# Queries, keys and gates by seven block products in a stage of their own, the attention and scan branches exchanged

## The chip, the cores and the metric

One core of a Trainium2 chip runs the whole program. The time is the device time of one execution in microseconds (us); the profile's span is the time from the first to the last instruction of one profiled execution. TensorE (PE in the profile) multiplies matrices, with PEld for the loading of its stationary operand; VectorE is DVE, ScalarE is ACT, GpSimd is POOL, and SyncE (SP) issues most DMA transfers. ScalarE and GpSimd issue some transfers as well.

## The reference

One decoder layer over 512 tokens of width 1024, in fp32: two parallel branches on the normalised input, merged by gates, then a SwiGLU feed-forward. Cut to what matters here:

```python
xn = rmsnorm(x, norm1_w)                       # (512, 1024)
q, k, v, z, xbc, dt_raw, gate_logits = split(xn @ w_in)   # 1536 | 1536 | 1536 | 2048 | 3072 | 32 | 2048
# attention branch: 3 dilation groups x 8 heads of 64, window of 128 steps
for g, (window, dil) in enumerate(((128, 1), (512, 4), (2048, 16))):
    o_g, lse_g = dilated_window_attention(q[:, :, g], k[:, :, g], v[:, :, g], bias[g], dil, window // dil)
attn = sum_g softmax_g(lse_g) * o_g            # (512, 512)
# scan branch (Mamba-2 SSD): 32 heads of 64 in 4 groups, state 128, chunks of 128
xbc = silu(causal_conv4(xbc)); dt = softplus(dt_raw + dt_bias)
y = ssd_chunked_scan(xs, dt, -exp(a_log), B, C) + xs * d_skip
ssm = grouped_rmsnorm(y * silu(z)) * ssm_norm_w
gates = sigmoid(gate_logits)                   # two of width 1024
merged = gates[0] * (attn @ w_attn_branch) + gates[1] * (ssm @ w_ssm_branch)
h = x + merged @ w_out
h = h + (silu(g) * u) @ w_ffn_out              # g, u = split(rmsnorm(h, norm2_w) @ w_ffn_in)
return rmsnorm(h, final_norm_w)
```

## The kernel before

Everything is held transposed: features on the 128 partitions, the 512 tokens along a row. To keep fp32 accuracy in a faster matmul format, each operand is split into a high part (rounded copy, made by ScalarE) and a low part (the difference, made by VectorE); a product is then three matmuls, high x high, high x low and low x high. This is `project` (L238): one block of 128 output features, 8 input blocks of 128, 24 matmuls of 128x512 into one PSUM bank. `values` (L311) does the same for V with tokens on the partitions: a group of 512 features takes 4 chunks (`c`) of 4 token blocks (`tt`), 6 matmuls each.

Weights stream through `Weights` (L45): a list of chunks in the order of use (`_chunk_plan`, L1204), loaded two chunks ahead by SP, split one chunk ahead (`fill`, L71: high part on ScalarE L81, low part on VectorE L82), with three buffers for raw, high and low parts.

The order of the work, by stage:

1. Start (to about 52 us). x is loaded, split unnormalised (`xu`), and V of group 0 is made from it, scaled per token when evicted (`keep`, L482). Woven between its token blocks by the table `at`: column sums, the root, its spread over rows (`first_rows`), the step sizes (`steps` L418, `steps_by_token` L429), the normalised input `xn` (`normalised`, L466). Then the first B and C blocks. In this stage the instructions of TensorE, VectorE and ScalarE keep the order in which they are written.
2. Scan (about 52 to 399 us). Four groups; in each a B and a C block, then four times an X and a Z block. `pair` (L547) is the scan of two heads and advances step by step at hooks: `project` calls one at its middle and one at its end. After group 2 come eight half blocks of the scan's output projection, `ssm_half(j, 0)`; after group 3 V of group 1.
3. V of group 2, the second halves `ssm_half(j, 1)`, then attention (about 499 to 677 us): for each of four pairs of heads, six blocks (query and key for three groups), whose results are split straight out of PSUM, and `softmax_pair` (L717), a generator of six steps: scores of group 0; scores of groups 1 and 2 and an exchange of row maxima through DRAM; exponentials and an exchange of sums; transposes (two steps); products with V. It advances at the end of each block. Eight gate blocks follow, and eight times a gate block and an attention branch block (four input blocks), which give `merged`.
4. The output projection, and the feed-forward's input: `Pairs` (L92) does two blocks of 128x1024 weights at once as a 2x2 arrangement of submatrices with seven products instead of eight (a Strassen-Winograd scheme): the tokens' halves and the features' halves give eight right-hand factors (`B11` to `B12`, `T1` to `T4`), the weights' halves and their sums (`sums13`, `sums24`) the left ones. Each product is 12 matmuls of 128x256. Low parts of unsummed weights are made by an accumulating DMA that GpSimd issues (`added`, L116): ScalarE writes the negated high part, the transfer adds the weights from DRAM. Then the feed-forward's output and the last norm.

Outside the hand-ordered parts a planner orders each engine's instructions by priority of writing and readiness, on its own estimate of durations; buffers are given out from pools and wait for their last readers. The lines of the start that the change's weave replaces:

```python
at = {(1, 1): column_sums, (1, 2): first_root, (2, 0): first_rows,
      (2, 1): lambda: (normalised(range(0, 4)), steps()),
      (2, 3): lambda: (steps_by_token(), normalised(range(4, 6))),
      (3, 1): lambda: normalised(range(6, 8)),
      (3, 3): lambda: ([next(chain) for _ in range(6)], nc.sync.dma_start(v_t[0], v0))}
```

Of the kernel before, what the change touches and what calls it, by code (L numbers as in the profile page):

```python
# [9 lines left out]
F32 = mybir.dt.float32  # L10
# [18 lines left out]
OUT_ORDER = (0, 4, 1, 5, 2, 6, 3, 7)  # L29

# [14 lines left out]
class Weights:  # L45


    def __init__(self, nc, pool, chunks, dma_ahead=2, split_ahead=1):
        self.nc, self.pool, self.chunks = nc, pool, chunks
        self.da, self.sa = dma_ahead, split_ahead  # L50
        self.i = self.loaded = self.split = 0
        self.raw, self.parts = {}, {}
# [18 lines left out]
    def fill(self, ahead=None, between=None):  # L71
        self.load(ahead)
        while self.split < min(len(self.chunks), self.i + (self.sa if ahead is None else ahead) + 1):
# [5 lines left out]
            for ks in self.pieces(i, kt):  # L79
                cs = slice(ks.start * n, ks.stop * n)  # L80
                self.nc.scalar.activation(hi[:, cs], r[:, cs], AF.Copy)  # L81
                self.nc.vector.tensor_sub(lo[:, cs], r[:, cs], hi[:, cs])  # L82
                if between:
                    between.pop(0)()
# [84 lines left out]
def trunk(ctx: ExitStack, tc: tile.TileContext, xT, w_in, w_v, w_dt, w_attn, w_ssm, w_out, w_fi, w_fo,  # L169
# [41 lines left out]
    wst = Weights(nc, wp, _chunk_plan(w_in, w_v, w_attn, w_ssm, w_out))  # L211
# [26 lines left out]
    def project(ps, rhs, first=True, last=True, at=None, w=wst):  # L238
        h, l, kt = w.next()
        for k in range(kt):  # L240
# [4 lines left out]
            if at is not None:  # L245
                if k in at:
                    at[k]()
            elif k == 3 and kt == KD:
                hook(False)
        if at is None:  # L250
            hook(True)
# [38 lines left out]
    def rel_rows(pool):  # L290

        tiles = [[pool.tile([P, S], F32, tag=f"sbr{2 * g + i}", name=f"rel{i}_{g}") for i in range(2)] for g in range(3)]
        for g in range(3):
            nc.gpsimd.dma_start(tiles[g][0][:33, : LREL[g]], oneh_d[:, OREL[g] : OREL[g] + LREL[g]])
        yield
        for g in range(3):
            (oneh, rv), n = tiles[g], LREL[g]
# [31 lines left out]
    sbr_cm = tc.tile_pool(name="sbr", bufs=1, reuse_waits="tile")  # L329
    sbrp = sbr_cm.__enter__()  # L330
# [3 lines left out]
    hcw = ssc.tile([P, P], F32, name="hcw")[:, :96]  # L334
    hcb = ssc.tile([P, 96], F32, name="hcb")[:, :24]
    relb = ssc.tile([33, 32], F32, name="relb")[:, :24]
    dt, la, te, eE = [ssc.tile([P, P], F32, name=n) for n in ("dt", "la", "te", "eE")]
# [4 lines left out]
    v_t = [v.rearrange("(c p) d -> p c d", p=P) for v in v_d]  # L342

    xn_cm = tc.tile_pool(name="xn", bufs=1, reuse_waits="tile", side="right")
    xnp = xn_cm.__enter__()

    order = tc.manual_schedule(engines={mybir.EngineType.PE, mybir.EngineType.DVE, mybir.EngineType.Activation})
    order.__enter__()
    with tc.tile_pool(name="s0", bufs=1, reuse_waits="tile") as s0:
        xt = [s0.tile([P, S], F32, name=f"x{k}") for k in range(KD)]  # L350
        xu = [tuple(s0.tile([P, S], F32R, name=f"xu{n}{k}") for n in "hl") for k in range(KD)]
        v0 = s0.tile([P, NCH, S], F32, name="v0")
        laf = s0.tile([32, S], F32, name="laf")
        t128 = s0.tile([P, S], F32, name="t128")
        ssum = s0.tile([P, S], F32, name="ssum")
        col = s0.tile([P, 32], F32, name="col")
        v, ab, e, ri, ss, s2, h, dta = [s0.tile([P, P], F32, name=f"c{i}") for i in range(8)]
        ax = s0.tile([P, 32], F32, name="ax")
        wd = s0.tile([P, KD, 32], F32, name="wd")
        sid = s0.tile([P, 64], F32, name="sid")  # L360
        rb1 = s0.tile([P, S], F32, name="rb1")
# [20 lines left out]
        act.activation(v[:, :NCH], mhalf, AF.Exp)  # L382
# [26 lines left out]
        ch = lambda t: t.rearrange("p (c h) -> p c h", h=32)  # L409
# [19 lines left out]
        def steps_by_token():  # L429
# [3 lines left out]
            for c in range(NCH):  # L433
                ev.scalar_tensor_tensor(v[:, c * 32 : c * 32 + 32], pt[:, c * 64 : c * 64 + 32], r1[0][:, c : c + 1],
                                        par("dtb", 0, 32), op0=ALU.mult, op1=ALU.add)

        def softplus():
            ev.scalar_tensor_tensor(ab, v, -1.0, v, op0=ALU.mult, op1=ALU.max)
            act.activation(e, ab, AF.Exp, scale=-1.0)
            act.activation(ax, par("alog", 0, 32), AF.Exp)  # L440
            yield
            ev.tensor_scalar(v, v, 0.0, None, op0=ALU.max)
            yield
            ev.tensor_scalar(ri, e, 2.0, None, op0=ALU.add)
            yield
            ev.reciprocal(ri, ri)
            yield
            ev.tensor_mul(ss, e, ri)
            yield
            ev.tensor_mul(s2, ss, ss)  # L450
            yield
            ev.tensor_scalar(h, s2, 1.0 / 15, None, op0=ALU.mult)
            for c in (13, 11, 9, 7, 5, 3):
                yield
                ev.scalar_tensor_tensor(h, h, 1.0 / c, s2, op0=ALU.add, op1=ALU.mult)
            yield
            ev.scalar_tensor_tensor(h, h, 1.0, ss, op0=ALU.add, op1=ALU.mult)
            yield
            ev.scalar_tensor_tensor(dt, h, 2.0, v, op0=ALU.mult, op1=ALU.add)
            yield  # L460
            ev.scalar_tensor_tensor(ch(dta), ch(dt), -1.0, ax.unsqueeze(1).to_broadcast([P, NCH, 32]), op0=ALU.mult, op1=ALU.mult)

        xn = []
        xm, todo = {}, []

        def normalised(ks):  # L466
            for k in ks:
                xm[k] = s0.tile([P, S], F32, tag="xm", name=f"xm{k}", bufs=3)
# [3 lines left out]
                xn.append((hi, lo))  # L472
                act.activation(hi, xm[k], AF.Copy)
                todo.append(k)
                while len(todo) > (k < KD - 1):
                    i = todo.pop(0)
                    (gp if i % 2 else ev).tensor_sub(xn[i][1], xm[i], xn[i][0])
# [4 lines left out]
        def keep(tt):  # L482
            act.activation(v0[:, tt, :], pv[tt], AF.Copy, scale=r1[0][:, tt : tt + 1])

        def decays():
            pl = bank()
            mm(pl[:, :P], tri, dta)
            mm(pl[:, P : 2 * P], ones, dta, start=False)
            act.activation(la, pl[:, :P], AF.Copy)
            act.activation(eE, pl[:, P : 2 * P], AF.Exp)  # L490
            ev.tensor_sub(te, pl[:, P : 2 * P], la)
            act.activation(te, te, AF.Exp)

        def decay_rows():
            pf = bank()
            for c in range(NCH):
                pe.transpose(pf[:32, c * P : c * P + P], la[:, c * 32 : c * 32 + 32], ident)
            act.activation(laf, pf[:32, :], AF.Copy)
            gp.dma_start(la_d, laf)
            dump("dt", dt)  # L500
            dump("la", laf)

        chain = softplus()
        at = {
            (1, 1): column_sums,
            (1, 2): first_root,
            (2, 0): first_rows,
            (2, 1): lambda: (normalised(range(0, 4)), steps()),
            (2, 3): lambda: (steps_by_token(), normalised(range(4, 6))),
            (3, 1): lambda: normalised(range(6, 8)),  # L510
            (3, 3): lambda: ([next(chain) for _ in range(6)], nc.sync.dma_start(v_t[0], v0)),
# [3 lines left out]
        pb0 = project(bank("mm"), xn, at={0: lambda: [None for _ in chain]})  # L515
        pc0 = project(bank("mm"), xn, at={4: decays, 7: decay_rows})
    order.__exit__(None, None, None)

    holder = {}
# [18 lines left out]
    with tc.tile_pool(name="sp", bufs=1, reuse_waits="tile") as sp:  # L538
# [109 lines left out]
        for g in range(NG):  # L648
# [14 lines left out]
            if g == 0:  # L663
                slow.append(rel_rows(sbrp))
# [646 lines left out]
```

## Time and profile before

| | us |
|---|---|
| median of three runs | 1147.26 (1146.73 to 1152.67) |
| profiled execution | 1150.79 |
| its span | 1149.0 |
| PE busy | 1132.8 |
| DVE busy | 715.3 |
| ACT busy | 569.9 |
| POOL busy | 181.6 |

The mean granted TensorE clock is 0.996. PE's busy time is 99% of the span; matmuls are pipelined, so busy means that one was under way, not that the array was full. The DMA engines moved 142.35 MB, a mean of 124 GB/s. Rows of busy time by stage have the stretch, its length, then for each engine busy us and the number of instructions, the granted clock, the share of the 16 DMA engines' time and GB/s.

### The profile page before, as it was taken

What the parts mean: (1) busy time and instruction counts of PE and PEld (TensorE: products, weight loads), DVE (VectorE), ACT (ScalarE), POOL (GpSimd) and SP (SyncE); (2) the same over time, 40 slices, a digit from 0 to 9 for tenths busy, and PEclk for the clock granted to TensorE, in tenths of its full rate; (3) what the DMA queues carried; (4) which work ended last, traced back from release to release, by engine and by line L of the source; (5) the groups of instructions that cost most, each with busy time, mean ns of one, the idle gap of its engine ahead of it and who ended that gap; (6) DMA issues with size and microseconds to landing.
All of it is one profiled execution on the core that took longest, in us unless ns stands there. A gap on an engine that the chain in (4) does not pass through costs nothing.

```text
span 1149.0 us, 17104 instructions
## 1 busy us (share of the span) xinstructions
PE 1132.8 (99%) x6636; PEld 969.5 (84%) x6636; DVE 715.3 (62%) x1253; ACT 569.9 (50%) x997; POOL 181.6 (16%) x169
## 2 busy tenths in 40 slices
PE   9999999999999999999999999999999999999996
PEld 6777888878888788888888888888999999988886
DVE  5777897873579333455564534478888777773222
ACT  5555565554345331336536533356767667663321
POOL 3214313222013300011211100000111111100001
PEclk9999999999999999999999999999999999999999
DMA  6343333233332373332333224345688888844322
GB/s 220 130 149 98 121 94 111 92 111 110 92 92 74 110 256 96 106 93 75 93 85 83 63 90 123 112 151 171 148 184 186 191 193 186 172 129 129 101 65 74
DMA packets 51521, 142.35 MB, mean 124 GB/s; under 512 B 6439, under 2 KB 13119, under 8 KB 51184
## 3 DMA queue, kind: packets, MB, share of 16 engines
q1 hardware_dynamic: 42096, 120.90, 33.9%
q0 software_dynamic: 6896, 16.04, 8.4%
q10 hardware_dynamic: 2448, 4.32, 1.3%
q8 instruction: 52, 0.85, 0.3%
q14 instruction: 29, 0.24, 0.1%
HBM read 133.76 MB, written 7.48 MB: 123 GB/s over the span
## 4 chain that ended last, share of the span: by engine, by line
PE 91%; DVE 4%; DMA 2%; ACT 1%; issue 1%; POOL 0%; SPq 0%; ACTq 0%; DVEq 0%; POOLq 0%
PE mm L179 74%; PE aux L179 15%; PE aux L182 2%; DVE wlo L82 1%; DMA x<-xT 0%; DMA lab<-la_d 0%; DVE frl L950 0%; DMA h_d<-h 0%; ACT whi L81 0%; DVE fS_lo L138 0%; DMA fa<-w_fi 0%; DVE xm L469 0%; DVE h L958 0%; POOL n2r L273 0%; DVE fA_lo L131 0%
## 5 line engine op out<-in xcount | busy, mean ns | idle before, releaser
L82 DVE TENSOR_TENSOR wlo<-wraw,whi 128x1024 fp32r<-128x1024 f32 (+2 forms) x156 | 185.7, 1195 | 185.3 <-ACT whi L81 185.1
L81 ACT ACTIVATE whi<-wraw 128x1024 fp32r<-128x1024 f32 (+2 forms) x156 | 152.2, 981 | 267.1 <-PE mm L179 238.1
L179 PE MATMUL mm<-xnh,whi 128*128 128x512 f32 x640 | 251.8, 393 | 1.4 <-DVE acc L530 1.3
L179 PE MATMUL mm<-xnh,wlo 128*128 128x512 f32 x640 | 252.6, 395 | 0.0
L179 PE MATMUL mm<-xnl,whi 128*128 128x512 f32 x640 | 251.1, 392 | 0.0
L179 PEld LDWEIGHTS mm<-xnh,whi 128*128 128x128 f32 x640 | 120.3, 188 | 27.3 <-ACT ce L562 1.7
L179 PEld LDWEIGHTS mm<-xnh,wlo 128*128 128x128 f32 x640 | 120.2, 188 | 26.9 <-issue 2.7
L179 PEld LDWEIGHTS mm<-xnl,whi 128*128 128x128 f32 x640 | 120.2, 188 | 24.9 <-issue 1.2
L179 PE MATMUL mm<-hhl,whi 128*128 128x512 f32 (+1 forms) x171 | 62.6, 366 | 0.6 <-DVE hhl L259 0.6
L179 PE MATMUL mm<-hhh,whi 128*128 128x512 f32 (+1 forms) x171 | 62.8, 368 | 0.2 <-ACT hhh L258 0.2
L179 PE MATMUL mm<-hhh,wlo 128*128 128x512 f32 (+1 forms) x171 | 62.3, 365 | 0.0
L121 POOL DMA_DIRECT2D fD_lo<-w_fi x22 | 19.1, 866 | 246.3 <-DVE h L958 135.8
L563 POOL TENSOR_TENSOR ce<-ce,Cf 128x768 f32<-128x768 f32 x16 | 34.7, 2173 | 140.9 <-ACT ce L562 78.2
L530 DVE SCALAR_TENSOR_TENSOR acc<-mm,hcw,acc 128x511 f32<-128x511 f32 (+2 forms) x72 | 53.2, 743 | 1.0
L138 DVE TENSOR_TENSOR fS_lo<-s,fS_hi 128x1024 fp32r<-128x1024 f32 x44 | 52.0, 1217 | 0.0
L179 PE MATMUL mm<-ssml,whi 128*128 128x512 f32 x128 | 50.2, 392 | 0.0
L179 PE MATMUL mm<-ssmh,wlo 128*128 128x512 f32 x128 | 50.1, 392 | 0.0
L179 PE MATMUL mm<-ssmh,whi 128*128 128x512 f32 x128 | 49.9, 390 | 0.0
L179 PE MATMUL mm<-frh,fS_hi 128*128 128x256 f32 x176 | 49.4, 281 | 0.5 <-ACT c L1031 0.5
L179 PE MATMUL aux<-frh,fS_hi 128*128 128x256 f32 x176 | 49.4, 280 | 0.0
L179 PE MATMUL aux<-frl,fS_hi 128*128 128x256 f32 x176 | 49.1, 279 | 0.0
L179 PE MATMUL aux<-frh,fS_lo 128*128 128x256 f32 x176 | 49.1, 279 | 0.0
(320 smaller groups left out, 2571.1 us busy)
## 6 DMA issues: line engine op xcount, KB each, us to landing
wraw<-w_in SPq DMA_DIRECT2D x80, 512.0 KB, 3.6
fb<-w_fi SPq DMA_DIRECT2D x22, 512.0 KB, 3.7
fa<-w_fi SPq DMA_DIRECT2D x22, 512.0 KB, 5.0
fA_lo<-w_fi POOLq DMA_DIRECT2D x19, 512.0 KB, 5.8
lab<-la_d SPq DMA_DIRECT2D x16, 512.0 KB, 3.7
wraw<-w_ssm SPq DMA_DIRECT2D x16, 512.0 KB, 3.8
wraw<-w_fo SPq DMA_DIRECT2D x15, 512.0 KB, 3.6
wraw<-w_v SPq DMA_DIRECT2D x11, 512.0 KB, 3.7
```

The source lines that it names most:

```text
L81: self.nc.scalar.activation(hi[:, cs], r[:, cs], AF.Copy)
L82: self.nc.vector.tensor_sub(lo[:, cs], r[:, cs], hi[:, cs])
L121: self.nc.gpsimd.dma_start(lo.rearrange("p (k n) -> p k n", n=P), src, accum_op=ALU.add)
L138: self.nc.vector.tensor_sub(lo, t, hi)
L179: pe.matmul(out, lhsT, rhs, start=start, stop=stop, skip_group_check=True)
L182: pe.transpose(out, src, ident)
L530: ev.scalar_tensor_tensor(acc[:, d:], ps[:, : S - d], hcw[:, t * 4 + 3 - d : t * 4 + 4 - d], acc[:, d:], op0=ALU.mult, op1=ALU.add)
L563: gp.tensor_mul(ce, ce, Cf[:, P:].unsqueeze(1).to_broadcast([P, 2, S - P]))
```

## The change

- Queries, keys and gates leave `project`. They are 20 pairs (12 of a query and a key block, 8 of the two gates' blocks) in a new loop with the feed-forward's `Pairs`, `product` and `head`, seven products of 12 matmuls a pair, between the start and attention. Only TensorE's order is written out there. Results go to DRAM: queries and keys already split and permuted (`qk_d`, 4 x 512 a partition), gates after their tanh (`gate_d`, 2 x 512).
- The start makes V of groups 0 and 1 from the unnormalised input. `normalised` now writes a column's low part right after its high part, all on VectorE; `factors` makes the token factors T1 to T4. Three of V's chunks get their low parts by accumulating DMA. The first B and C blocks leave the start. The softplus of the steps moves into the pairs' loop.
- Attention comes before the scan. `load_heads` brings a head pair's queries and keys back with 16 transfers; V of group 2, six of the sixteen Z blocks (`EARLY_Z`, results kept in DRAM) and the first B and C blocks are woven with it; `attention` advances the four generators at every hook, two of them interleaved.
- The scan has no Z blocks for tiles 8 to 13; the first half of its output projection comes at tiles 10 and 11; the attention branch's blocks are at its end, with the gates loaded from DRAM; the second half of the output projection gives `merged`.

The diff, cut to its core (moved code is left out):

```diff
+EARLY_Z = range(8, 14)
+HALF_AT = {10: (0, 1, 2), 11: (3, 4, 5, 6, 7)}
...
-            for ks in self.pieces(i, kt):
+            if i in self.added:
+                self.nc.scalar.activation(hi, r, AF.Copy)
+                self.nc.scalar.activation(lo, hi.bitcast(F32), AF.Copy, scale=-1.0)
+                self.nc.gpsimd.dma_start(lo.rearrange("p (k n) -> p k n", n=n), self.chunks[i], accum_op=ALU.add)
+            for ks in self.pieces(i, kt) if i not in self.added else ():
...
-    wst = Weights(nc, wp, _chunk_plan(w_in, w_v, w_attn, w_ssm, w_out))
+    wst = Weights(nc, wp, [w_v[g, c] for g in (0, 1) for c in range(4)], added=(5, 6, 7))
...
         def normalised(ks):
             for k in ks:
-                xm[k] = s0.tile([P, S], F32, tag="xm", name=f"xm{k}", bufs=3)
+                xm[k] = s0.tile([P, S], F32, tag="xm", name=f"xm{k}", bufs=4)
                 ev.scalar_tensor_tensor(xm[k], xt[k], par("n1", k), rb1, op0=ALU.mult, op1=ALU.mult)
...
                 act.activation(hi, xm[k], AF.Copy)
-                todo.append(k)
-                while len(todo) > (k < KD - 1):
-                    i = todo.pop(0)
-                    (gp if i % 2 else ev).tensor_sub(xn[i][1], xm[i], xn[i][0])
+                ev.tensor_sub(lo, xm[k], hi)
+
+        def factors(p):
+            f = s0.tile([P, 4, HS], F32, tag="tf", name=f"tf{p}", bufs=2)
+            (b11, b12), (b21, b22) = [[xm[k][:, :HS], xm[k][:, HS:]] for k in (p, p + 4)]
+            hi, lo = tw[p]
+            ev.tensor_sub(f[:, 0], b11, b12)
+            ev.scalar_tensor_tensor(f[:, 1], b22, -1.0, f[:, 0], op0=ALU.mult, op1=ALU.subtract)
+            ev.tensor_sub(f[:, 2], b22, b12)
+            ev.scalar_tensor_tensor(f[:, 3], f[:, 1], -1.0, b21, op0=ALU.mult, op1=ALU.subtract)
+            act.activation(hi, f, AF.Copy)
+            ev.tensor_sub(lo, f, hi)
...
+            (0, 3): column_sums,
+            (1, 0): first_root,
+            (1, 2): first_rows,
+            (1, 3): steps,
+            (2, 0): lambda: normalised((0, 4)),
+            (2, 2): lambda: (steps_by_token(), normalised((1, 5))),
+            (3, 0): lambda: (factors(0), wst.fill(1)),
+            (3, 2): lambda: (normalised((2,)), factors(1)),
+            (3, 3): lambda: (nc.sync.dma_start(v_t[0], v01), wst.fill(1)),
...
+            (0, 0): lambda: normalised((6,)),
+            (0, 1): lambda: (factors(2), wst.fill(1)),
+            (0, 3): lambda: normalised((3, 7)),
+            (1, 1): lambda: (factors(3), ev.tensor_copy(r1[1], r1[0])),
+            (1, 2): lambda: wst.fill(1),
+            (1, 3): first_pairs,
+            (2, 3): lambda: holder["fi"].first(0, add=False),
+            (3, 0): lambda: holder["fi"].sums13(0),
+            (3, 1): lambda: holder["fi"].load(1),
+            (3, 2): lambda: holder["fi"].first(1, add=False),
+            (3, 3): lambda: (holder["fi"].sums24(0), holder["fi"].sums13(1), nc.sync.dma_start(v_t[1], v01)),
...
+    def finished(n, i, src):
+        if n < 12:
+            if i == 0:
+                outs[n] = p1.tile([P, 4, S], F32R, tag="st", name=f"st{n}", bufs=2)
+            st = outs[n]
+            parted((st[:, 2 * i], st[:, 2 * i + 1]), src, 1.0 if i else -0.125, n % 3)
+            if i:
+                nc.sync.dma_start(qk_d[n], outs.pop(n).bitcast(F32))
+        else:
...
+            act.activation(st[:, i], src, AF.Tanh, scale=-0.5 if i else 0.5)
+            if i:
+                nc.sync.dma_start(gate_d[n - 12], outs.pop(n)[:, :2])
...
+    for n in range(NP):
...
+        r, q, c1, c5 = heads.pop(n)
...
+        fi.last(n)
...
+        product(s_, fi, factor, n, "a12", B21, True, True)
+        ev.tensor_add(ga[:, half[0]], s_, c1)
...
+        fi.sums13(n + 1)
+        product(r, fi, factor, n, "s2", T2, False, False)
+        u2 = copied(p1, r, "u2", n)
+        if before:
+            finish1(*before)
+        product(q, fi, factor, n, "s4", B22, False, True)
+        ev.tensor_add(ga[:, half[1]], q, u2)
+        fi.load(n + 2)
+        fi.sums24(n + 1)
+        product(r, fi, factor, n, "s3", T3, False, False)
...
+        finished(n, 0, ga)
...
+        quick.append([attention()])
         for c in range(4):
             values(pv, 2, c, xn, stage2)
+        for t in EARLY_Z:
+            ps = project(bank("mm"), xn)
...
+            nc.sync.dma_start(zs_d[t], z)
+        pb0 = project(bank("mm"), xn)
+        pc0 = project(bank("mm"), xn)
+        drain()
...
+                if t in EARLY_Z:
+                    nc.sync.dma_start(zs[t], zs_d[t])
...
+                for j in HALF_AT.get(t, ()):
+                    first_half(j)
...
         for j in range(KD):
+            t = sp.tile([P, 2, S], F32, tag="lab", name=f"gt_{j}", bufs=2)
+            nc.sync.dma_start(t, gate_d[j])
+            ev.scalar_tensor_tensor(sbr[j], t[:, 0], 1.0, sbr[j], op0=ALU.add, op1=ALU.mult)
+            pa = project(bank("mm"), attn)
+            ev.scalar_tensor_tensor(t[:, 1], t[:, 1], 1.0, pa, op0=ALU.add, op1=ALU.mult)
+            ev.tensor_add(sbr[j], sbr[j], t[:, 1])
```

800 lines of the change are left out of this document (436 added, 364 removed).

## The prediction

> **What bounds the kernel now.** I read the page's head and its chain first, then busy time by stage, then the chain in order of time.
>
> ```profile
> span 1149.0 us, 17104 instructions
> PE 1132.8 (99%) x6636; PEld 969.5 (84%) x6636; DVE 715.3 (62%) x1253; ACT 569.9 (50%) x997; POOL 181.6 (16%) x169
> PE 91%; DVE 4%; DMA 2%; ACT 1%; issue 1%; POOL 0%; SPq 0%; ACTq 0%; DVEq 0%; POOLq 0%
> ```
>
> TensorE is busy 99% of the span and carries 91% of the chain. So matmul time removed is time saved, unless TensorE then waits for what it did not wait for before. The stages (columns: length, then busy us of PE, PEld, DVE, ACT, POOL, granted clock, DMA share, GB/s) tell how near the others are:
>
> ```profile
> 0.00:39.00 39.00, 36.19 (x168) 26.47 (x169) 23.33 (x38) 20.36 (x31) 13.75 (x15) 0.96 0.47 162
> 52.00:288.70 236.70, 235.36 (x1337) 188.88 (x1336) 182.35 (x336) 128.92 (x253) 65.32 (x40) 1.00 0.35 113
> 499.00:677.50 178.50, 178.50 (x1062) 151.34 (x1061) 94.95 (x240) 91.37 (x212) 23.67 (x34) 1.00 0.30 78
> 825.00:995.00 170.00, 170.00 (x1446) 170.00 (x1445) 136.11 (x228) 120.28 (x176) 29.57 (x35) 1.00 0.83 188
> ```
>
> Rows two and three are the scan and the attention with its projections: VectorE is 77% busy in the one, 53% in the other. The last is the feed-forward, which already uses the seven products: weight loads fill it wholly, VectorE is at 80%, ScalarE at 71%, the DMA engines at 83%. The new stage has that shape.
>
> **Part 1: seven products for eight, a gain of 20.0 us.**
>
> ```profile
> 673.18 76.22 PE mm L179 x336
> 841.87 1.41 PE aux L179 x12
> 851.76 1.41 PE aux L179 x12
> 583.47 5.49 PE mm L179 x24
> 628.33 5.49 PE mm L179 x24
> ```
>
> Chain rows: start, length, what. 336 matmuls in 76.22 us are 0.2268 us each, so a block of 24 takes 5.44 and the two blocks of a pair 10.89. A feed-forward pair, 7 x 12 = 84 matmuls of half the columns, takes 851.76 - 841.87 = 9.89. Half the columns cost 0.118, not 0.113, since each also loads weights. So a pair saves 1.00, not an eighth of 10.89, and 12 pairs of queries and keys with 8 of gates save 20.0. Values, Z, B, C, X, the branch and output blocks keep their count and are costed at nothing where they only move.
>
> **Part 2: the start, a loss of 17 us.** Before, four chunks of values end at 39.09 and two ordinary blocks follow. After, group 1's four chunks run there (21.8 us, to 60.9), and in their cover VectorE and ScalarE, in the written order, must make the normalised columns, the four factors and the weight parts.
>
> ```profile
> 27.53 1.92 PE L179 MATMUL aux<-x,wd 128*32 128x512 f32 x16
> 39.09 0.39 PE L179 MATMUL mm<-xnh,whi 128*128 128x512 f32 x1
> 23.07 1.23 DVE L82 TENSOR_TENSOR wlo<-wraw,whi 128x1024 fp32r<-128x1024 f32 x1
> 26.88 1.42 DVE L469 SCALAR_TENSOR_TENSOR xm<-x,prm,rb 128x512 f32<-128x512 f32 x2 [2.58 <-ACT rb L480]
> 28.33 0.69 DVE L477 TENSOR_TENSOR xnl<-xm,xnh 128x512 fp32r<-128x512 f32 x1
> 33.81 0.73 DVE L434 SCALAR_TENSOR_TENSOR c<-aux,n1r,prm 128x32 f32<-128x32 f32 x4 [1.81 <-PE aux L179]
> 899.82 0.41 DVE L1103 TENSOR_TENSOR us<-us,g 128x256 f32<-128x256 f32 x1
> 27.66 1.29 ACT L473 ACTIVATE xnh<-xm 128x512 fp32r<-128x512 f32 x2 [0.82 <-DVE xm L469]
> 31.97 0.58 ACT L422 ACTIVATE t<-aux 128x512 f32<-128x512 f32 x1
> 36.43 1.04 ACT L81 ACTIVATE whi<-wraw 128x1024 fp32r<-128x1024 f32 x1
> fA_lo<-w_fi POOLq DMA_DIRECT2D x18, 512.0 KB, 5.9
> ```
>
> The row at 33.81 shows the order binding: VectorE sits idle 1.81 us for TensorE with four columns still to normalise. Where before the low part of a column came after the next column's product, after it follows its own high part at once: 0.71 + 0.64 (ScalarE, VectorE waiting) + 0.69 and two hand-overs, 2.15 a column. A factor is 4 x 0.41, then the high part of 1024 (1.04), then the low (1.23): 4.1 with hand-overs.
> The walk: the steps' matmuls move up past two token blocks (2 x 1.36), so they end at 27.53 - 2.7 + 1.9 = 26.7, and ScalarE's copy of them (0.58) now stands ahead of a weight split (1.04 + 1.23). The first column starts near 29.6. Eight columns (17.2), four factors (16.4), the steps (0.73) and one split with its wait (1.7) end at 65.6, past 60.9. Worse, the parts of the last three value chunks are issued by ScalarE behind factors 0, 2 and 3 (two copies of about 1.05, then an accumulating transfer of 5.9 to landing). Chunk 6 stands behind the high part of factor 2, at 29.6 + 6 x 2.15 + 0.73 + 1.7 + 2 x 4.1 + 2.8 = 55.9, and lands at 63.9; TensorE wants it at 39.1 + 10.9 = 50. Chunk 7 lands near 72, so the values end near 77 instead of 60.9. Queued behind on ScalarE are the values' evictions and, behind these, the sums of the first two pairs: another 4 to 5 us before the second pair's first sum. The upper end is 21. The lower: VectorE never waits, 8 x 1.40 + 4 x 2.9 + 2.4 = 25 us from 29.6, done near 55, leaves about 3 for the sums. I take 17, near the upper end because the row at 33.81 is of that kind, less some for transfers that land sooner where DMA is at 0.47 than at 0.83.
>
> **Part 3: DMA in the pairs of queries and keys, a loss of 5 us.** Added on SP's queue: per such pair a store of 1.05 MB, per gate pair 0.52.
>
> ```profile
> q0 software_dynamic: 5115, 14.02, 47.9%
> q1 hardware_dynamic: 6018, 18.23, 33.8%
> 10.00:15.00 5.00, 5.00 (x16) 3.91 (x16) 4.74 (x6) 5.00 (x9) 2.97 (x2) 0.66 1.07 378
> 415.00:420.00 5.00, 5.00 (x24) 4.14 (x23) 0.75 (x1) 2.70 (x4) 0.00 (x0) 1.00 1.01 371
> ```
>
> The queue rows are of 825 to 1000 us. Of 9.89 us a pair, accumulation takes 47.9% (4.74) and loads 33.8% (3.34): 8.1. A store at 371 GB/s adds 2.8; at the loads' own rate (18.23 MB in 0.338 x 175 us, 308 GB/s) 3.4. That is 10.9 to 11.5 of DMA time, and a share of 1.07 is the highest shown: 10.2 at best, so 0.3 to 1.6 over TensorE's 9.89, or 4 to 19 over 12 pairs. Stores of 8 KB a row are nearest the 371 row: 10.9 / 1.05 = 10.4, thus 5 to 6, and I take 5. Gate pairs need about 9.5 and fit. A store queues ahead of the next pair's loads, which the sums on VectorE wait for. The rest of a pair's work is the feed-forward's: its tanh and two products give way to two splits of 512.
> The Trainium skill, "DMA: Bandwidth & Descriptors", the table at its head, gives HBM about 358 GB/s for one core. By that a pair's 2.9 MB need 8.1 us, the store hides and this part is 0; the trace differs on both counts, since loads ran at 371 and accumulation at 14.02 MB in 83.8 us, 167 GB/s.
>
> **Part 4: attention woven with other blocks, a loss of 3 us.**
>
> ```profile
> L780 ACT ACTIVATE L<-L,nm 128x256 f32<-128x256 f32 x32 | 15.8, 496 | 13.2 <-DVE nm L771 13.2
> L777 ACT ACTIVATE L<-L,nm 128x256 f32<-128x256 f32 x24 | 11.9, 497 | 0.0
> L777 ACT ACTIVATION_READ_ACCUMULATOR L<-L,nm 128x1 f32 x32 | 6.1, 190 | 0.0
> L780 ACT ACTIVATION_READ_ACCUMULATOR L<-L,nm 128x1 f32 x32 | 6.0, 187 | 0.0
> dscr<-d POOLq DMA_DIRECT2D x4, 4.0 KB, 1.7
> d1n<-dscr POOLq DMA_DIRECT2D x4, 4.0 KB, 3.7
> L913 DVE SCALAR_TENSOR_TENSOR sbr<-g,sbr 128x512 f32<-128x512 f32 x6 | 4.1, 685 | 0.0
> ```
>
> A head pair took 628.33 - 583.47 = 44.86 with six blocks of 5.44, so its own TensorE work is 12.2. After, 12 blocks (65.3) and four head pairs (48.8) share 114 us; the row of the stage before has 178.5. ScalarE's exponentials are 39.8 / 4, 10 us a head pair, under the 28 that one now gets, so no engine becomes the bound. But the walk has 28 steps for 24 hooks. The last pair's exponentials come half a block before the end; then 10 us, 1.7 + 3.7 for the sums' round trip, and its products. Cover: half a block (2.7), X and Z of the scan (10.9), its own transposes (3): 16.6 against 15.4 and hand-overs. Ends 0 and 15; I take 3, with the 16 loads of each head pair that SP holds until single buffers come free: weights queue behind them.
>
> **Part 5: the scan, a loss of 3 us.** Six Z blocks leave it, eight branch half-blocks fill its end. There TensorE has 8 x 2.72 = 21.8; VectorE has 24 operations of 0.685 for the gates (16.4), 4.9 of half splits and about 10 for the last tile and its normalisation, so 10 too many. The next eight blocks (43.5 us) leave room to catch up. Ends 0 and 10; I take 3, since banks, not data, would hold TensorE. Four low parts move from POOL to VectorE and are in part 2; POOL's accumulations stand as in the feed-forward.
>
> **The sum.** -20.0 + 17 + 5 + 3 + 3 = +8. The profiled execution took 1150.79 (span 1149.0 and 1.8 around it), so 1158.8 there; the median of the runs shown is 1147.26, 3.5 lower, so 1155.
>
> **The rivals.**
> - *The start is covered* (faster): the transfers of chunks 5 to 7 arrive before TensorE asks. For it: ScalarE is 52% busy in the first row of stages, the transfers are its only work there that TensorE needs. Against it: the written order. Then 1155 - 17 = 1138. It decides once the start costs under 3.6 us, where the time passes 1141.5.
> - *The stores hide*: 1155 - 5 = 1150. For it: the 0.17 of idle DMA share. Against it: the 2.8 needed are more than 17% of 9.89. This is also the page's case.
> - *The stores cost their upper end*: 1.6 x 12 = 19, so 1169.
> - *The pairs save nothing*, held at 10.89 by waits in each: 1155 + 20 = 1175. Against it: the feed-forward holds 9.89 throughout.
> - *The clock falls in the waits at the start*: the row at 10 us shows 0.66 for 5 us after early waits, a loss of 1.7. Twice that is 1158. The Trainium skill, "TensorE: Matmul & The Clock Gate", section "HAM oscillation", has the clock halved after about 3.4 us without work, and waits of 5 and 7 us are forecast; no later row of this trace has one.
>
> **How the numbers follow.** Forecast 0.40, its own range 1148 to 1163; covered start 0.15; hidden stores 0.20; costly stores 0.10; clock 0.10; no saving 0.05. What a measurement of this kernel can tell from no change is about 0.5%, 5.7 us: 1141.5 to 1153. Faster: 0.15, a quarter of 0.20, a little of the forecast: 0.22. Same: most of the hidden stores and a third of the forecast: 0.30. Slower: 0.48. From the covered start to the costly stores the range is 1137 to 1170.
>
> **What the next profile would show.** Pairs at 9.89 for gates and near 10.4 for queries, DMA share near 1 there; values of group 1 taking nearer 35 than 22 us, TensorE waiting for accumulated parts of the values' weights; waits of a few us at the end of attention and of the scan. The prediction is wrong if group 1's values run without waits, or if query pairs also hold 9.89.

## The result: 1234.3 us, seven per cent slower

The changed kernel took 1234.34 us (median of 4 runs, 1226.32 to 1236.68), the kernel before, beside it, 1149.55 us: a ratio of 1.0725, 95% interval 1.0662 to 1.0787. The forecast was 1155, with a range from 1137 to 1170: the sign was right, the size was not. The head of the page after, its strip of 40 slices, and its chain:

```profile
span 1234.9 us, 19238 instructions
...
PE 1145.4 (93%) x7356; PEld 1006.0 (81%) x7356; DVE 791.1 (64%) x1413; ACT 657.1 (53%) x1146; POOL 198.5 (16%) x193
...
PE   8679999989967976999999998999999999999997
PEclk9879999999978987999999999999999999999999
DMA  5457999976788742233424322666487888844322
...
PE 59%; DMA 17%; DVE 11%; issue 5%; ACT 4%; SPq 1%; POOL 1%; DVEq 0%; ACTq 0%; POOLq 0%
```

TensorE carried 91% of the chain before; now it is 59%, and DMA 17%. A slice of the strip is 30.9 us. TensorE's share falls to 6 or 7 in two places, the slices to 93 us and those between 340 and 494 us, and in both the granted clock falls with it. The DMA row is at 9 between 123 and 247 us. The stages by windows (length, then busy us of PE, PEld, DVE, ACT, POOL, granted clock, DMA share, GB/s): values of two groups; the first pair; the other pairs; attention; scan.

```profile
0.00:79.50 79.50, 61.92 (x263) 46.42 (x264) 40.94 (x71) 37.14 (x51) 9.08 (x12) 0.89 0.51 151
79.50:100.50 21.00, 16.77 (x120) 16.22 (x119) 17.96 (x35) 11.04 (x19) 1.44 (x2) 0.84 0.46 141
100.50:309.50 209.00, 197.46 (x1601) 191.63 (x1600) 127.77 (x190) 144.72 (x228) 38.22 (x46) 1.00 0.89 239
309.50:485.50 176.00, 136.49 (x805) 112.57 (x804) 67.08 (x210) 67.94 (x179) 19.20 (x30) 0.86 0.68 183
485.50:834.00 348.50, 344.11 (x1904) 278.82 (x1905) 272.16 (x477) 175.45 (x343) 80.12 (x48) 0.99 0.38 121
```

What each would take with TensorE never waiting, by the durations of the trace before (0.2268 us for 512 columns, 0.1178 for 256, 12.2 us of own work in a head pair):

| stage | took | without waits | lost | forecast |
|---|---|---|---|---|
| values, groups 0 and 1 | 79.5 | 39.1 + 21.8 = 60.9 | 18.6 | 17 for this row |
| first pair | 21.0 | 120 x 0.1178 = 14.1 | 6.9 | and this one |
| other pairs | 209.0 | 1560 x 0.1178 + 23 x 0.2268 + 1.5 = 190.5 (about 1.5 for 14 small ones) | 18.5 | 5 |
| attention | 176.0 | 313 x 0.2268 + 4 x 12.2 = 119.8 | 56.2 | 3 |
| scan | 348.5 | 50 blocks, 272.2, and about 73.7 for the rest, as in the scan before | 2.6 | 3 |

The losses add up to 102.8; less the 20 that the pairs save that is 83. Measured, the merged output projection starts at 834.2 instead of 749.2, 85 later, and from there both kernels take 400 to 401 us. So the question is the attention first, then the pairs and the start.

**The start** went as the walk had it. Rows of the chain in order of time (start, length, what):

```profile
57.57 0.64 ACT xnh L459
58.23 0.69 DVE xnl L460
...
61.38 1.05 ACT whi L82
62.45 1.07 ACT wlo L83
...
63.80 8.94 DMA wlo<-w_v
...
72.88 5.68 PE mm L185 x17
```

ScalarE and VectorE pass columns and factors to each other in the written order; the parts of the last chunk come behind them, its accumulating transfer takes 8.94, lands at 72.7 (forecast "near 72") and TensorE starts then. That the landing fits within a us is in part luck: the transfer took 3.0 longer than the 5.9 of the walk, and started 2.3 earlier than the walk's 66.1 (72 less 5.9).

**The pairs.** DMA between 100 and 250 us: queues (packets, MB, share of 16 engines), and two kinds of transfers (count, KB, median us to landing).

```profile
q1 hardware_dynamic: 5922, 27.86, 54.7%
q0 software_dynamic: 4159, 11.09, 42.0%
...
qk_d<-st SPq DMA_DIRECT2D x12, 1024.0 KB, 5.4
fb<-w_in SPq DMA_DIRECT2D x14, 512.0 KB, 6.4
```

The engines are full: 54.7 + 42.0 = 97% of the time, of which the accumulating queue has 42% for 28% of the bytes. 14 pairs in 150 us make 10.4 us of DMA time for each, more than TensorE's 9.89.

**The attention.** What TensorE waited for between 309.5 and 486 us (total, times, longest):

```profile
PE mm L185 <- ACT whi L87: 14.3, 2, 8.2
PE mm L185 <- DVE acc L951: 9.0, 1, 9.0
PE aux L185 <- DVE m L842: 6.5, 4, 5.0
...
PE aux L185 <- DMA k<-qk_d: 2.7, 1, 2.7
```

Weight parts come too late (`whi`), then VectorE's convolution at the head of the scan (`acc`), then the row maxima (`m`). The chain behind the three (L857 loads keys and queries, L965 the rows of the scan, L838 stores the attention's output):

```profile
356.23 12.43 DMA k<-qk_d
368.68 0.44 SPq L857
...
371.55 6.55 DMA wraw<-w_in
378.13 1.06 ACT whi L87
...
431.10 7.46 DMA nscr<-m
...
440.28 5.55 DMA dscr<-d
...
478.70 0.32 SPq L838
...
479.11 4.30 DMA lab<-la_d
```

Keys of the next head pair take 12.43 us, SP then issues the weights that queue behind them, and they need 6.55: TensorE stands until 379.2. At 431 and 440 us small exchanges through DRAM are on the chain; at 479 the scan's rows, which VectorE takes between two steps of that convolution, could be loaded only once the last output store (478.7) had left SP. The waits by themselves, 39.5 us (176.0 less the 136.5 in which TensorE is busy), are not all. Windows of 5 us across the first of them:

```profile
345.00:350.00 5.00, 2.35 (x13) 2.07 (x12) 0.07 (x2) 0.00 (x0) 1.10 (x2) 0.58 0.82 216
350.00:355.00 5.00, 0.65 (x4) 0.36 (x2) 2.58 (x16) 0.00 (x0) 0.18 (x1) 0.50 0.99 285
355.00:360.00 5.00, 3.19 (x7) 2.08 (x8) 2.51 (x3) 2.11 (x2) 1.33 (x2) 0.50 1.05 336
360.00:365.00 5.00, 5.00 (x18) 3.95 (x17) 0.19 (x2) 0.00 (x0) 0.07 (x1) 0.71 1.06 181
```

The first wait for weights lasts 6.1 us and ends at 356.8. The granted clock is at 0.50 in both windows that hold it, and from 360 to 365 us 18 matmuls ran, where at full clock 22 of 512 columns fit. The Trainium skill, "TensorE: Matmul & The Clock Gate", section "HAM oscillation", has the clock halved by a gap of more than about 3.4 us. The trace agrees on the half (0.50 in this wait), not on the gap: the clock is at 0.58 already between 345 and 350 us, ahead of this wait, where TensorE's longest wait was 2.7 us (that for `k`).

### The profile page after: what moved, and what is told of

Same layout as the page of the kernel before. It is cut to its first block, busy times and chain, and to the rows that moved or that the text cites. A ratio compares the mean times of both kernels' runs of the same rounds, so it can differ in the third digit from the quotient of the medians.

```text
span 1234.9 us, 19238 instructions
## 1 busy us (share of the span) xinstructions
PE 1145.4 (93%) x7356; PEld 1006.0 (81%) x7356; DVE 791.1 (64%) x1413; ACT 657.1 (53%) x1146; POOL 198.5 (16%) x193
## 4 chain that ended last, share of the span: by engine, by line
PE 59%; DMA 17%; DVE 11%; issue 5%; ACT 4%; SPq 1%; POOL 1%; DVEq 0%; ACTq 0%; POOLq 0%
PE mm L185 44%; PE aux L185 14%; DMA fb<-w_in 7%; PE aux L188 1%; DVE wlo L88 1%; DVE fS_lo L144 1%; DMA nscr<-m 1%; DMA g<-gate_d 1%; DMA k<-qk_d 1%; DMA dscr<-d 1%; DVE s L154 1%; DMA mscr<-m 1%; DMA gt<-gate_d 1%; DMA wlo<-w_v 1%; SPq L857 1%
## 5 line engine op out<-in xcount | busy, mean ns | idle before, releaser
L88 DVE TENSOR_TENSOR wlo<-wraw,whi 128x1024 fp32r<-128x1024 f32 (+3 forms) x114 | 128.2, 1131 | 133.3 <-ACT whi L87 132.8
L87 ACT ACTIVATE whi<-wraw 128x1024 fp32r<-128x1024 f32 (+3 forms) x114 | 106.6, 945 | 176.9 <-PE mm L185 141.4
L185 PE MATMUL mm<-xnh,whi 128*128 128x512 f32 x352 | 140.9, 404 | 25.2 <-ACT whi L87 14.3
L185 PE MATMUL mm<-xnh,wlo 128*128 128x512 f32 x352 | 142.8, 407 | 0.1
L185 PE MATMUL mm<-xnl,whi 128*128 128x512 f32 x352 | 141.8, 403 | 0.0
L143 ACT ACTIVATE fS_hi<-s 128x1024 fp32r<-128x1024 f32 x84 | 87.0, 1051 | 40.8 <-DVE s L154 30.8
L185 PEld LDWEIGHTS mm<-xnh,whi 128*128 128x128 f32 x352 | 67.7, 193 | 41.0 <-ACT whi L87 15.1
L185 PEld LDWEIGHTS mm<-xnh,wlo 128*128 128x128 f32 x352 | 67.8, 193 | 16.5 <-issue 1.9
L185 PEld LDWEIGHTS mm<-xnl,whi 128*128 128x128 f32 x352 | 68.0, 193 | 14.8 <-issue 1.0
L951 DVE SCALAR_TENSOR_TENSOR acc<-mm,hcw,acc 128x509 f32<-128x509 f32 (+2 forms) x72 | 53.1, 743 | 1.4 <-ACT acc L949 0.6
```

Of the source, the lines that this page charges most:

```text
L143: self.nc.scalar.activation(hi, t, AF.Copy)
L185: pe.matmul(out, lhsT, rhs, start=start, stop=stop, skip_group_check=True)
L951: ev.scalar_tensor_tensor(acc[:, d:], ps[:, : S - d], hcw[:, t * 4 + 3 - d : t * 4 + 4 - d], acc[:, d:], op0=ALU.mult, op1=ALU.add)
```

## The experiments

Twelve kernels, each an edit of the changed one. Stage lengths are from the matmuls that bound the stages in each trace; the first column is the end of the values, the second from there to the last gate pair. Expectations that say 182 us for the attention count from its first block, at 303 us; the table's 176.0 counts from the last gate pair, at 309.5.

| edit | values end | pairs | attention | scan | median us | ratio to before |
|---|---|---|---|---|---|---|
| none | 79.3 | 230.2 | 176.0 | 348.7 | 1234.34 | 1.0725 [1.0662, 1.0787] |
| e1 fills | 66.9 | 235.2 | 176.7 | 354.1 | 1235.05 (one run) | |
| e2 start | 61.7 | 229.7 | 177.4 | 356.0 | 1223.43 | 1.0661 [1.0615, 1.0707] |
| e3 no accumulation | 78.4 | 219.3 | 174.7 | 350.2 | 1223.55 | 1.0659 [1.0601, 1.0718] |
| e4 stores on ScalarE | 78.2 | 229.2 | 172.7 | 353.7 | 1236.28 | 1.0779 [1.0737, 1.0821] |
| e5 one reload | 76.6 | 229.2 | 151.4 | 354.6 | 1215.02 | 1.0587 [1.0543, 1.0632] |
| e6 weights aside | 78.4 | 228.6 | 174.2 | 348.8 | 1233.39 | 1.0757 [1.0705, 1.0809] |
| e7 more Z | 78.6 | 231.6 | 194.8 | 341.1 | 1245.12 | 1.0855 [1.0798, 1.0911] |
| e8 joined | 61.1 | 218.9 | 170.2 | 354.2 | 1208.38 | 1.0530 [1.0492, 1.0569] |
| e9 joined, one reload | 61.9 | 219.8 | 148.6 | 353.2 | 1182.86 | 1.0290 [1.0266, 1.0315] |
| e10 joined, fewer Z | 61.6 | 218.0 | 156.8 | 369.8 | 1210.13 | 1.0537 [1.0517, 1.0558] |
| e11 no exchange | 78.6 | 231.3 | 154.7 | 349.7 | 1214.91 | 1.0569 [1.0511, 1.0626] |
| e12 joined, neither | 60.4 | 221.6 | 137.8 | 354.2 | 1175.28 | 1.0204 [1.0137, 1.0272] |

Intervals of single edits overlap with that of the changed kernel where the gain is about 1% (e2, e3); there the stage columns carry the verdict.

**e1, e2: the start.**

```diff
-  (3, 0): lambda: (factors(0), wst.fill(1)),
+  (3, 0): lambda: (wst.fill(1), factors(0)),   # e1: likewise the other two fills
-  ev.tensor_sub(lo, xm[k], hi)
+  lows.append(lambda ...: (gp if k < 4 else ev).tensor_sub(lo, xm[k], hi))   # e2: e1 and this,
+  settle(2)                                    # a low part two items after its high part
```

> Only the order at the start: the parts of the last three value chunks are issued before the factors and columns of their step, the low parts stay where they are. If the queue order on ScalarE alone made the three gaps at 43, 62 and 73 us, the values of group 1 end near 62 to 66 us (79.7 before this edit), and the rest of the loss comes back in the first two pairs, whose factors are then late: their first sums start no earlier than 80 to 85 us, and the kernel gains 3 to 8. If the transfers' own time made them, values end past 74 us and nothing is gained.

> The start alone is rearranged: the weight parts of the last three value chunks are issued before the columns and factors that share their step, and each low part is made two items after its high part, half of the columns' ones on GpSimd. Theory of the written order (part 2 of the prediction): the values of group 1 end near 61 to 66 us instead of 79.7, the gaps at 43, 62 and 73 us go, and the whole kernel is 14 to 19 us faster than the changed kernel. Rival, the transfers: the parts land no earlier because the accumulating queue is full there; values still end at 75 or later, gain under 5. Rival, given back later: values end near 62, but the pairs that follow are held by DMA and the gain on the whole is under 8.

Windows of e2 from the start to the end of the values:

```profile
0.00:61.90 61.90, 56.48 (x263) 43.12 (x264) 40.64 (x67) 36.76 (x51) 15.71 (x16) 1.00 0.63 194
```

The same 263 matmuls end 18 us earlier, with the clock at 1.00 instead of 0.89. So the written order made the waits; the transfers themselves do not take that long to arrive. With the fills alone (e1) values end at 66.9, 12.4 earlier and just past the forecast, but 5.0 come back in the pairs, whose factors are late, and 5.4 in the scan: of the 3 to 8 us expected nothing is left. With e2 the pairs and the attention keep their length, the scan takes 7.3 more, and 10.9 of the 17.6 remain in the median. The first theory holds for the place; the gain on the whole lies between it and the third, given back in the scan and not in the pairs.

**e3, e4: the pairs, bytes against order.**

```diff
-  fi.first(n + 1)
+  fi.first(n + 1, add=fi is not holder["fi"])     # e3
-  nc.sync.dma_start(qk_d[n], ...)
+  nc.scalar.dma_start(qk_d[n], ...)               # e4, and gate_d
```

> In the stage of queries, keys and gates the low parts of the first operand are subtracted by VectorE and not sent through an accumulating transfer: 0.5 MB less for the GpSimd queue in each pair, 1.2 us more for VectorE, 1 us less for ScalarE. Theory of throughput (part 3 of the prediction, sized too low): query pairs fall from 10.0 to 11.9 us to 9.9 to 10.2, DMA share in 100 to 250 us falls from 0.93-1.0 to under 0.9, the kernel gains 8 to 15 us. Rival, order: the stores and loads that wait on SP's queue hold the pairs; the loads land as late, gain under 4. Rival, VectorE becomes the bound: pairs at 11 or more, no gain or a loss.

> The stores of queries, keys and gates are issued on ScalarE's queue; nothing else moves. Theory of SP's order: SP no longer stands 86.7 us for the stores' sums, the next pair's weight loads land earlier, pairs fall to near 9.9 to 10.2, the kernel gains 8 to 20 us. Theory of throughput: the same bytes go through the same 16 engines, DMA share stays 0.93 to 1.0 in 100 to 250 us, the query pairs stay at 10.5 to 11 and the gain is under 4. Third: ScalarE, held by the stores' waits, makes its splits later, a loss of 3 to 10.

The same 150 us of DMA, first e3, then e4 (q10 is ScalarE's queue):

```profile
q1 hardware_dynamic: 6293, 29.23, 56.7%
q0 software_dynamic: 2180, 3.83, 15.7%
```

```profile
q0 software_dynamic: 4192, 11.17, 41.6%
q1 hardware_dynamic: 4032, 14.68, 30.2%
q10 hardware_dynamic: 1993, 13.58, 23.7%
```

Without the larger accumulation the engines are 72% full, the pairs fall by 10.9 us, and the kernel by 10.8. With the stores on another queue the sum is again 96% and the pairs are as long. So between 100 and 250 us, most of which is query pairs, transfers through full DMA engines held the pairs, not what stood in SP's queue. (e3 also takes 1 us a pair from ScalarE; it was busy 111 of these 150 us, so that is the lesser suspect, but it was not tried by itself.)

In the last gate pairs the DMA engines are not full, and the pairs are longest there. Two windows of the changed kernel; then, between 95 and 300 us, what SP's weight loads (L119) wait for longest, and VectorE's wait for the load of a pair's second block, `fb`:

```profile
253.00:264.00 11.00, 10.20 (x82) 9.43 (x81) 5.24 (x10) 7.27 (x13) 2.15 (x3) 1.00 0.79 216
264.00:277.00 13.00, 10.24 (x86) 10.03 (x85) 6.08 (x10) 7.38 (x13) 1.74 (x2) 1.00 0.76 182
...
SPq L119 <- DVE ga L677: 41.9, 14, 7.4
...
DVE s L153 <- DMA fb<-w_in: 53.8, 17, 6.9
```

SP issues such a load only behind VectorE's work on the pair before, at 254.1 and 265.8; it lands 5.9 and 6.7 us later, and only then do VectorE's sums start. A round of one load and the work behind it takes 11.7, longer than TensorE's 9.89, with a fifth to a quarter of the DMA time unused. In e3 the same load lands after 3.9 us between 240 and 300 us (median; 6.1 in the changed kernel), and the last pairs are at 9.99. Such rounds are there in the query pairs too; with the engines full, the record does not tell the two apart. A further buffer, so that `fb` is loaded earlier, was not tried.

**e5, e6, e7: the attention.**

```diff
-  heads_of[load] = load_heads(load)
+  heads_of[load] = heads_of[0]                    # e5
-  self.nc.sync.dma_start(v[:, ks, :], src[:, ks, :])
+  (self.nc.scalar if i < self.aside else self.nc.sync).dma_start(...)   # e6, aside=14
-  nc.sync.dma_start(attn_d[hp], t)
+  gp.dma_start(attn_d[hp], t)                     # e6
-  EARLY_Z = range(8, 14)
+  EARLY_Z = range(4, 16)                          # e7
```

> Head pairs 1 to 3 use the queries and keys of head pair 0, so that three quarters of the reloads from DRAM are left out (some 9 MB); the same matmuls, exponentials and blocks run. The attention took 182 us where its matmuls fill 126. Theory of the reloads (their bytes, and weights queued behind them on SP): the attention falls by 30 to 50 us, to 132 to 152. Theory of the chain (scores, maxima, exponentials, round trips of the sums, one head pair after another, with 14 blocks as cover): it falls by less than 12, and the gaps of the last 45 us stay.

> The weight loads of the attention's stage are issued on ScalarE's queue and the stores of the attention's output on GpSimd's; the same bytes move. Theory of SP's order: in the attention weights no longer stand behind head loads that wait for their buffers, nor the scan's first loads behind the last output store; the gaps at 356.8 and 379.2 (6.4 and 8.4 us, TensorE waiting for weight parts) and the one of 9.1 at 485.5 go, and the attention (182 us) falls by 15 to 25. Theory of bytes: weights and head loads share the same DMA engines at a share of 0.9, the first two gaps stay within 4 us of what they were in sum, only the last one goes; gain 5 to 10. Theory of the chain: what goes from these gaps returns in the waits of the last 45 us, gain under 4.

> Twelve instead of six Z blocks are made in the attention's stage, taken out of the scan (6 x 5.44 = 32.6 us of matmul moved). Theory of too little cover: the attention's length stays near 182 us plus at most 12, since the blocks fill the waits of its last 45 us, and the scan falls by some 25 to 33; the kernel gains 12 to 25. Theory of bytes and queue order: the six blocks bring 6 x 0.5 MB of weights and 1.5 MB of stores into the stretch where the DMA share is 0.9, the attention grows by 25 or more and the gain is under 5. Third: the scan, which loses cover for VectorE's work (87 us busy in 100), starts to wait; attention near 190, scan shorter by less than 20, gain under 8.

Without three quarters of the reloads the attention is 24.6 us shorter: less than the one theory said, more than the other. The small exchanges, which had not been touched, became faster too; first the changed kernel's rows in the attention (count, KB, us to landing), then e5's:

```profile
nscr<-m POOLq DMA_DIRECT2D x4, 4.0 KB, 6.2
m1n<-nscr POOLq DMA_DIRECT2D x4, 4.0 KB, 6.4
```

```profile
nscr<-m POOLq DMA_DIRECT2D x4, 4.0 KB, 4.2
m1n<-nscr POOLq DMA_DIRECT2D x4, 4.0 KB, 2.3
```

e6 gains 1.8 us there and 1 in all, inside the spread: weights on a queue of their own share the engines with the reloads, and what the first waits lose, the later ones take (a new one of 9.3 us that ends at 384). In e7 the stage's windows are

```profile
310.00:505.00 195.00, 165.31 (x951) 135.10 (x950) 78.04 (x222) 77.45 (x192) 19.28 (x30) 0.92 0.67 190
505.00:846.00 341.00, 322.96 (x1760) 260.29 (x1761) 270.26 (x464) 165.93 (x331) 80.39 (x48) 0.95 0.37 119
```

Of 32.6 us of blocks moved, 13.8 filled waits of the attention (it grew by 18.8), but the scan fell by 7.6 only and waits itself now (clock 0.95). Cover taken from the scan is missed there: the third theory has the place, though the kernel does not gain a little but loses 10.8.

**e11: the exchange.**

```diff
-  gp.dma_start(nat(mscr[hp]), m0)                 # and the five other transfers
+  m0p, m1n = m0, m1                               # likewise d1n = d1
```

> The changed kernel without the exchange of row maxima and sums through DRAM (24 small transfers of the softmax, 5.8 + 4.6 and 6.2 + 6.4 us, then 4.2 + 3.1, for each head pair): each layout uses its own maxima and sums, which leaves that part of the computation out. All matmuls, exponentials, reloads and blocks stay. Theory of the chain: a head pair's steps follow each other through these trips, so the attention (176 us from the last gate block on) falls by 12 to 30. Theory of the reloads: the next head pair's loads and the weights behind them set the pace, the trips lie beside them, and it falls by less than 6.

```profile
309.90:464.70 154.80, 128.61 (x806) 107.89 (x805) 65.82 (x210) 68.31 (x180) 3.50 (x6) 0.92 0.72 208
```

The reloads are all there (208 GB/s), and the attention is 21.3 us shorter. The chain of a head pair through DRAM counts nearly as much as the reloads.

**e8, e9, e10, e12: joined.** e8 is e2, e3 and the output store on GpSimd's queue; e9 adds e5's edit, e12 e5's and e11's; e10 is e8 with `EARLY_Z = range(8, 10)`.

> Joined: the start rearranged with the lagged low parts, no accumulating transfers in the new stage, and the attention's output stores on GpSimd's queue. If the causes found are separate and add, the stages take what each edit alone gave: values to 62 us, query pairs near 10.0, the 9 us gap ahead of the scan down to 2 to 7; the sum is 11 + 11 + 3 = 25 us under the changed kernel, about 1209. Rival, given back: the scan, which grew from 349 to 354-356 us wherever the attention ended earlier, takes another 5 and the pairs' time returns as waits in the attention; then 1215 to 1222. Neither theory has it below the kernel before.

> The joined version with head pair 0's queries and keys used for all head pairs (three quarters of the reloads left out). If the reloads' bytes cost 25 us in the attention independent of the rest, the attention falls to 140 to 152 and the kernel to 1185 to 1190. If they only mattered because the accumulating transfers and the late start crowded the same stretch, it gains under 10 on the joined version.

> The joined version with two instead of six Z blocks in the attention's stage, four more in the scan (21.8 us of matmul moved back). Theory of a scan short of cover: the scan's gaps in its last 90 us (9 to 13 us) close, it grows by only 9 to 14, and the attention, whose length is set by loads and chain, falls by 5 to 15; the kernel stays within 5 us or gains up to 5. Theory of too little cover in the attention: it falls by less than 5, the scan grows by 15 to 22, the kernel loses 10 to 17.

> The joined version with one head pair's reloads and without the exchange through DRAM: what is left of the attention's loss once both suspects are gone. Its matmuls fill 120 us; with reloads taken out it was 149. If reloads and trips make up the whole, it falls to 125 to 135. If it stays above 143, the rest is neither: weight parts that arrive late, the wait of 7 us ahead of the scan, and the lower clock after each of them.

The attention's window in e8, and in e12:

```profile
280.00:450.30 170.30, 135.82 (x806) 112.48 (x804) 67.16 (x210) 68.39 (x180) 21.39 (x34) 0.89 0.69 189
```

```profile
282.00:419.90 137.90, 126.09 (x806) 106.37 (x804) 65.88 (x210) 68.30 (x180) 5.72 (x10) 0.96 0.50 159
```

e8 came at 1208.4 where the sum said 1209: start and pairs are separate causes and add. In e9 the reloads are worth 21.6 us of attention on top, as the first theory had it, and 25.5 of the total (1182.9, a little below its 1185). Reloads and exchange together take off 32.4 (170.2 to 137.8), not 24.6 + 21.3: they overlap, since the reloads are part of what makes the exchange slow. What is left, 18 us over the 119.8, is for the most part the wait ahead of the scan (6.7), one of 3.7, and the clock behind them. The 137.8 lies between the two lines of e12's expectation (135 and 143), so neither was met. In e10 the attention fell by 13.4 and the scan grew by 15.6: the total is the same within the spread, so between two and six early Z blocks the number does not matter, and with twelve (e7) the kernel loses.

No version beats the kernel before. The best with the whole computation, e8, is 5.3% slower than it (interval 4.9 to 5.7); e12, which leaves out reloads and exchange, is still 2.0% slower (1.4 to 2.7).

## Why the prediction went wrong

**Part 1, the pairs, held.** In e8 the pairs past the first take 196.5 us where 190.5 are matmul; the scheme brings its 1.00 a pair, and the 20 us are in the result (102.8 lost less 20 are 83, and 85 were measured).

**Part 2, the start: mechanism right, 17 against 25.5.** The values ended at 79.5 (forecast 77). The term was too small by what it left out of its own walk, the first pair's sums (forecast 4 to 5, of which little was kept; 6.9), and by the clock (0.89 and 0.84 in its two windows). Its upper end of 21 was too low. What it was worth is less: e2 gains 10.9, since the scan gives some back.

**Part 3, DMA in the pairs: 18.5 against 5, inside its ends of 4 to 19.** The ends counted the query pairs alone, which lost 10.4, so that it lies inside is luck. The price of a query pair was near: 10.4 forecast, 10.4 us of DMA time measured; accumulation ran at 11.09 MB in 63 us, 176 GB/s (167 forecast). The pairs themselves took 10.8 (129.1 for twelve). The step that failed is "gate pairs need about 9.5 and fit": it set DMA time against TensorE's time, and not the round of a load and the work behind it, 11.7. The seven periods between the starts of the eight gate pairs' last products took 78.3 us together (11.1 to 13.0 for the first five), where the feed-forward's 9.89 make 69.2, and 71.3 in e3; so accumulation costs more there, 7.0, than in the twelve query pairs, 4.5 (129.1 to 124.6). What e3 leaves, 5.9 in the query and 2.1 in the gate pairs, no edit took away. The rival that the stores hide, also by the 358 GB/s of the Trainium skill's "DMA: Bandwidth & Descriptors", table at its head, fell: 261 GB/s went through at a share of 0.97, the hardware queue alone at 340 in its own time.

**Part 4, attention: the step that failed, 3 (end 15) against 56.** The forecast compared matmul (114) and ScalarE's time (10 of 28 us) with the stage's length, found "no engine becomes the bound", and priced only the tail. It named the reloads' queue, but gave it no time of its own, and of the exchange it priced only the last head pair's sums, 1.7 + 3.7. Before, six blocks lay beside each head pair and TensorE never waited, so the exchange was hidden; the reloads are new, since the queries and keys had come straight out of PSUM. After, 14 blocks lie beside four head pairs instead of 24 (the forecast counted 12), and neither is hidden. That the stage kept its length, 176 against 178.5, is chance: before, matmul filled it, and now it falls with the reloads and the exchange. Reloads are worth 24.6 of the 56 (e5), the exchange 21.3 (e11), both together less than their sum. Of the 9.0 ahead of the scan only 2.3 went when the output's store left SP's queue (e8):

```profile
PE mm L185 <- DVE acc L959: 6.7, 1, 6.7
```

In e8 the chain across this wait has no transfer left in it; it is ScalarE's and VectorE's work on the attention's last result and then the convolution, which were not tried in another order.

**Part 5, the scan: 2.6 against 3, in part by luck.** The forecast's wait, for VectorE behind on the gates, is not there in the changed kernel. Its two waits are 2.1 for VectorE's operand of the last tile (`xw`) and 1.9 for the attention's output, which is split again after its load from DRAM.

**The clock**, a rival at 3.4 us, acts in the attention: the same matmuls are busy 136.5 us at a clock of 0.86 and 126.1 at 0.96 (e12). It comes on top of the waits and is no case apart.

Open: why the scan takes 353 to 356 us in seven of these kernels (e1, e2, e4, e5, e8, e9, e12) and 349 to 350 in the changed kernel and in e3, e6 and e11, though the scan is written alike in all of them. In all seven TensorE waits 2.1 to 5.6 us at its end for VectorE's products with the gates (5.2 in e8), which is the mechanism of part 5; in the changed kernel it does not, and in e3, e6 and e11 for 1.2 to 1.6. What makes VectorE late in the seven was not tried.

## What to carry to other kernels

When blocks are taken from beside a chain of dependent steps, compare the chain's own length, with every round trip and reload in it, with the work that is left beside it, not only each engine's sum. In a stage where TensorE never waits, the trace does not show how much of its cover that chain needs. Price DMA time of a stage against its length with all queues added, and take accumulating transfers at their own, lower rate. Where a load is issued only behind the work of the round before, add its landing to that work: the round can be too long though the DMA engines are not full.

## What the hardware showed that was not expected

Half-column matmuls have two rates. The feed-forward between 900 and 950 us, in the changed kernel and then in e2, where nothing of that stage differs:

```profile
900.00:950.00 50.00, 49.93 (x424) 49.73 (x423) 41.33 (x70) 36.08 (x55) 8.62 (x10) 1.00 0.82 192
```

```profile
900.00:950.00 50.00, 50.00 (x444) 50.00 (x443) 42.08 (x71) 37.43 (x55) 9.52 (x11) 1.00 0.84 198
```

444 instead of 424 matmuls in 50 us, at the same granted clock: 0.113 us each instead of 0.118. Of the traces, e2 and e9 have the faster rate through the whole feed-forward. The prediction had put the 0.118 down to weight loads; with the same loads 0.113 is possible, so that reason is not shown. It makes some 8 us of a profile's total, which is why the stages are compared here. And the same transfer of 4 KB took 2.3 us (median) in e5 and 6.4 in the changed kernel, which differ only in the reloads that the DMA engines carried beside it.
